# Eight gate tiles of each layer: copied out of PSUM by ScalarE and multiplied with the norm's row on GpSimd, in place of one multiplication on VectorE

## The chip, the cores and the metric

The kernel runs on one core of one Trainium2 chip. The metric is the time of one execution on the device in microseconds (us), given as the median of several runs. The profile speaks of five engines: PE (TensorE's matmuls; PEld is its loading of weights), DVE (VectorE), ACT (ScalarE), POOL (GpSimd) and SP (SyncE, which only issues DMAs here).

## The reference

Two layers, each over 512 tokens of width 1024, all in float32. What matters of one layer:

```
h = rms_norm(x, norm_mix[l])
z = h @ w_in[l]
qa, ka, va, qi, ki, wi, cq, ckv, kr, ga, gb = split_cols(z)
...
y_a = sparse_indexed_attention(qa, ka, va, qi, ki, wi, rel_bias, topk)
...
y_b = latent_attention(qb, kb, vb)
gate_a = jax.nn.sigmoid(ga + b_gate[l, :D_MODEL])
gate_b = jax.nn.sigmoid(gb + b_gate[l, D_MODEL:])
merged = gate_a * (y_a @ w_proj_a[l]) + gate_b * (y_b @ w_proj_b[l])
x = x + merged @ w_out[l]
```

Then comes a convolutional feed-forward block. Mixer a picks 128 keys for each query (top-k over an indexer's scores); mixer b is dense latent attention. Both have eight heads. The second gate, gb, has 1024 channels, that is eight tiles of 128 channels by 512 tokens, and is used only after both mixers.

## The kernel before

Everything is held transposed: channels on the 128 partitions, the 512 tokens along the free dimension. Each float32 factor is split into two float32r parts, high and low, and a product is three matmuls (high by high, high by low, low by high). A `dense` call (L511 to L526) makes one tile of 128 output channels: 24 matmuls into one PSUM bank of tag D, of which there are two, and then a function that empties the bank.

A weight tile arrives raw by SP's DMA (`wr`). ACT casts it to the high part `wh` (L172). The low part `wl` is made in one of two ways: by a subtraction on DVE (L184), or, for gb, ga, kv, uq and some others, by ACT writing the negated copy (L200) and POOL issuing a DMA that adds the raw tile (L201).

The norm is applied late. The matmuls run on x times the gain; the factor of each token, `nrm.row`, the same in all partitions, comes in when a bank is emptied. For both gates that is L686 in `evac_gate`: one DVE multiplication of the bank with the row, written to an SBUF tile. (A branch for gb, switched by `GBL`, is off.) Biases and sigmoid follow at L1254, after mixer a's last head; L906 then multiplies with mixer b's projection.

One generator, `mix_dense`, makes all the projections of a layer in a fixed order: indexer, latents, four gb tiles (`GB_0`), the two groups of mixer b's keys, values and queries (`attn_b`), four more gb tiles, group 0 of mixer a, and so on. The heads of the mixers are woven with it: each step of a head lets this filler advance by a rate. Steps that should come some ticks later are put off by `later(n, f)`; a tick is one step of a generator. Beside that, `top_k` (L991) runs on DVE, alternating MAX8 (L998) and MATCH_REPLACE8 (L1005) over three score tiles, 48 rounds of each a layer. POOL turns the queries of mixer b by their rotary angles (L868 to L874) and adds the bias tiles for mixer a (L1078).

A list scheduler then sets the order in each engine's queue, by a model of when operands are ready and by program order as priority; an instruction marked `keep_in_program_order` is kept in its place in the program. On the chip each queue runs strictly in that order, and an instruction at its head that waits holds what is behind it.

The functions that the change touches are `evac_gate` (L680), the loop over gb at the end of `mix_dense`'s part for mixer b (L893 to L899), and the lines ahead of the sigmoids (L1249 to L1254).

Of the kernel before, what the change touches and what calls it, by code (L numbers as in the profile page):

```python
# [15 lines left out]
OP = mybir.AluOpType  # L16
# [45 lines left out]
PBO = 0  # L62
# [11 lines left out]
SU2 = '12'  # L74
PCH = 2000
GA_0 = 0
GBL = 0
LAG_D = [2, 4, 5, 7, 8, 10, 12]
WPOOL = []
WMOD = 1  # L80
# [153 lines left out]
def trunk(ctx: ExitStack, tc: tile.TileContext, xT, wd, vecs, rel, rot_n, onehot, outT):  # L234
# [12 lines left out]
    def slot(s, dt=F32):  # L247
        return sb.tile([128, 512], dt, name=nm(s), tag="slot", bufs=N_SLOTS)
# [15 lines left out]
    def bank(tag):  # L264
        return ps.tile([128, 512], F32, name=nm(tag), tag=tag, bufs=N_PS[tag])

    mm = nc.tensor.matmul
    V, A, G = nc.vector, nc.scalar, nc.gpsimd
# [5 lines left out]
    def later(n, f):  # L274
        if n == 0:
            f()
        else:
            pending.append((clock[0] + n, f))
# [110 lines left out]
    def vc(l, i, n=1):  # L389
        return vec[:, l * NV + i:l * NV + i + n]  # L390
# [120 lines left out]
    def dense(kt, parts, xh, xl, evac, c0=0, last=True, tag="D", t0=0):  # L511
        h, o = parts
        p = bank(tag)
        c = lambda k: slice(c0 + k * 128, c0 + (k + 1) * 128)
        if "d" in LO:
            seq = [(h[:, c(k)], x[k]) for k in range(kt) for x in (xh, xl)] + [(o[:, c(k)], xh[k]) for k in range(kt)]
        else:
            seq = [q for k in range(kt) for q in ((h[:, c(k)], xh[k]), (h[:, c(k)], xl[k]), (o[:, c(k)], xh[k]))]
        for n, (w, x) in enumerate(seq):
            if n and n % 3 == 0:  # L520
                yield
            mm(p[:, t0:], lhsT=w, rhs=x[:, t0:], start=n == 0, stop=n == len(seq) - 1, skip_group_check=True)  # L522
        if last:
            W.ahead()
        evac(p)
        yield  # L526

    def rows(name, grp, nrm, evac):

        pp = [bank("D").rearrange("p (t c) -> p t c", t=2) for _ in range(2)]  # L530
        for half in range(2):
            h, o = W.get(name, 2 * grp + half)
            for b in range(2):
                for t in range(2):
                    ts = slice((2 * b + t) * 128, (2 * b + t + 1) * 128)
                    c = lambda k: slice(k * 256, (k + 1) * 256)
                    xs = [(nrm.h[4 * half + k][:, ts], nrm.o[4 * half + k][:, ts]) for k in range(4)]
                    if "r" in LO:
                        seq = [(x, h[:, c(k)]) for k in range(4) for x in xs[k]] + [(xs[k][0], o[:, c(k)])
                                                                                for k in range(4)]  # L540
                    else:
                        seq = [q for k in range(4) for q in ((xs[k][0], h[:, c(k)]), (xs[k][1], h[:, c(k)]),
                                                             (xs[k][0], o[:, c(k)]))]
                    for n, (x, w) in enumerate(seq):
                        mm(pp[b][:, t, :], lhsT=x, rhs=w, start=n == 0 and half == 0 and t == 0,  # L545
                           stop=n == 11 and half == 1, skip_group_check=True)
                        if n == 5 or (n == 11 and t == 0):
                            yield
                if b == 1:
                    W.ahead()  # L550
                if half:
                    evac(b, pp[b])
                yield
# [3 lines left out]
    late = []  # L557

    def mix_dense(l, nrm):
# [119 lines left out]

        def evac_gate(name, m, p):  # L680
            g = slot(name)
            if name == "gb" and GBL and not PBO:
                A.copy(g, p)
                late.append((g, nrm.row))
            else:
                tables["v"] = V.tensor_tensor(out=g, in0=p, in1=nrm.row, op=OP.mult)  # L686
            st[name][m] = g
# [89 lines left out]
        def evac_va(grp, b, p):  # L777
            for t in range(2):
                j = 2 * b + t
                d = st["va"][j][grp] = slot("va", F32R)  # L780
                d = d.rearrange("p (h c) -> p h c", c=128)
                split_into(d[:, :, 0:64], d[:, :, 64:128], p[:, t, :].rearrange("p (h c) -> p h c", c=64),
                           nrm.rstd[:, j:j + 1])

        def attn_a(grp):
            yield from heads("qa", grp, None)
            yield from heads("ka", grp, gab[:, 2 * l:2 * l + 1])
            yield from rows("va", grp, nrm, lambda b, p: evac_va(grp, b, p))
            done.add(f"a{grp}")
# [103 lines left out]
        for m in range(8):  # L893
            if m == GB_0:
                yield from attn_b(0)
            if m == GB_1:
                yield from attn_b(1)
            yield from dense(KD, W.get("gb", m), nrm.h, nrm.o, lambda p, m=m: evac_gate("gb", m, p))
        yield from attn_a(0)  # L899
        for m in range(GA_0):  # L900
            yield from dense(KD, W.get("ga", m), nrm.h, nrm.o, lambda p, m=m: evac_gate("ga", m, p))
# [15 lines left out]
        for m in range(GA_0, 8):  # L917
            yield from dense(KD, W.get("ga", m), nrm.h, nrm.o, lambda p, m=m: evac_gate("ga", m, p))
# [241 lines left out]
    nrm = Norm(gain0)  # L1160
# [10 lines left out]
    for l in range(DEPTH):  # L1171
        st.clear()
        done.clear()
        fl = Filler(mix_dense(l, nrm))
        if l:
            for k in range(SQ_DOWN, KD):
# [70 lines left out]
                     lambda h: lambda j: st["va"][j][h // 4][:, (h % 4) * 128:(h % 4 + 1) * 128], each_a, "a")  # L1247
        fl.until("ga")
        gb = st["gb"]  # L1249
        for g, row in late:  # L1250
            V.tensor_tensor(out=g, in0=g, in1=row, op=OP.mult)
        late.clear()
        for m in range(0 if PBO else 8):
            table(AF.Sigmoid, gb[m], gb[m], bias=vc(l, V_GATE + 8 + m))  # L1254

# [28 lines left out]
        nrm = Norm(vc(l, V_FFN, KD))  # L1284
# [203 lines left out]
        nrm = nxt  # L1488
# [103 lines left out]
```

## Time and profile before

| what | value |
|---|---|
| median of 3 runs | 1543.3 us (1542.56 to 1543.44) |
| profiled execution, its own time | 1542.06 us |
| its span, first to last instruction | 1540.3 us |
| around the span | 1.76 us |
| mean granted TensorE clock | 1.000 |
| gb tiles, both layers | 16 |

The profile's page gives for each engine the busy time and its share of the span. A group of instructions is shown by line, engine and operation, what it writes and reads, and the count, then its busy time, the mean of one in nanoseconds, the engine's idle time before it, and what ended that. A row of the timeline has start, length, engine and line; an "x2" at its end means two in a row merged. A row of waits has who waited for whom, the total, the times and the longest. Line numbers of the kernel after are 4 higher than before between L899 and L1249.

### The profile page before, as it was taken

The page shows a single profiled execution, that of the slowest core. Times are in us where ns is not written, and L with a number is a line of the kernel's source. Part 1 is how long each engine was busy: PE and PEld are TensorE (multiplying, and loading weights), DVE is VectorE, ACT ScalarE, POOL GpSimd, SP SyncE. Part 2 cuts the span into 40 slices and gives each one's busy share as a digit, 9 for nine tenths or more (in the row PEclk, how much of TensorE's full clock was granted, in tenths as well). Part 3 has the DMA queues.
Part 4 walks back from the last instruction along what each step waited for, and adds up shares of the span by engine and source line. Part 5 has one row for each costly group of instructions (what it writes and reads, how often), then busy time and mean ns, then how long its engine had stood idle before and what let it go on. Part 6 is the DMA issues. An engine that isn't in the chain of part 4 may idle for free.

```text
span 1540.3 us, 23962 instructions
## 1 busy us (share of the span) xinstructions
PE 1530.1 (99%) x8662; PEld 1336.5 (87%) x8662; DVE 1123.0 (73%) x2301; ACT 947.0 (61%) x1555; POOL 392.7 (25%) x578
## 2 busy tenths in 40 slices
PE   9999999999999999999999999999999999999999
PEld 7887999888888898889998889998888888988899
DVE  7799988666476693447979999886574757835587
ACT  6856677773567545664457577686635765466642
POOL 1243003300011431124602520124001115321255
PEclk9999999999999999999999999999999999999999
DMA  7564134734488438883454641356435883488823
GB/s 277 132 156 123 56 96 97 191 112 134 120 181 200 108 117 213 190 181 93 139 184 110 157 110 56 104 125 168 139 96 142 186 185 95 147 201 193 176 86 109
DMA packets 72983, 219.02 MB, mean 142 GB/s; under 512 B 8528, under 2 KB 10104, under 8 KB 72736
## 3 DMA queue, kind: packets, MB, share of 16 engines
q1 hardware_dynamic: 53824, 149.15, 30.8%
q0 software_dynamic: 18432, 65.28, 23.6%
q10 hardware_dynamic: 608, 3.05, 0.6%
q8 instruction: 68, 1.11, 0.3%
q14 instruction: 51, 0.42, 0.1%
HBM read 143.77 MB, written 6.84 MB: 98 GB/s over the span
## 4 chain that ended last, share of the span: by engine, by line
PE 81%; DVE 9%; ACT 2%; issue 1%; POOL 0%; ACTq 0%
PE D L522 35%; PE T L522 15%; PE D L545 6%; PE L L1385 5%; PE T L1385 4%; PE D L1385 3%; PE Y L1043 2%; PE Y L1385 2%; PE T L1036 2%; PE L L522 2%; DVE sc L1005 1%; DVE m L998 1%; PE L L323 1%; PE L L322 1%; DVE mx L1130 1%
## 5 line engine op out<-in xcount | busy, mean ns | idle before, releaser
L172 ACT CAST wh<-wr 128x1024 fp32r<-128x1024 f32 (+1 forms) x206 | 212.2, 1033 | 161.2 <-PE D L522 67.8
L201 POOL DMA_DIRECT2D wl<-wr x128 | 110.8, 878 | 631.0 <-ACT wl L200 602.3
L522 PE MATMUL D<-hxh,wh 128*128 128x512 f32 (+1 forms) x448 | 176.5, 394 | 0.0
L522 PE MATMUL D<-hxl,wh 128*128 128x512 f32 (+1 forms) x448 | 175.2, 391 | 0.0
L200 ACT ACTIVATE wl<-wr 128x1024 fp32r<-128x1024 f32 (+2 forms) x128 | 132.2, 1035 | 47.2 <-PE D L522 25.0
L190 ACT CAST wh<-wr 128x896 fp32r<-128x896 f32 x88 | 82.8, 942 | 103.7 <-POOL wr L214 62.5
L1078 POOL TENSOR_TENSOR P<-M,sel 128x128 f32<-128x128 f32 (+1 forms) x64 | 54.4, 903 | 272.8 <-DMA M<-skewd 157.6
L522 PE MATMUL D<-hxh,wl 128*128 128x512 f32 (+1 forms) x448 | 119.2, 393 | 0.0
L545 PE MATMUL D<-wh,hxh 128*128 128x256 f32 x384 | 113.9, 297 | 0.0
L214 POOL TENSOR_TENSOR wr<-wr 128x256 f32<-128x256 f32 x88 | 93.9, 1068 | 61.9 <-DVE wr L213 43.3
L545 PE MATMUL D<-wl,hxh 128*128 128x256 f32 x384 | 109.1, 284 | 0.0
L195 DVE TENSOR_TENSOR wl<-wr,wh 128x896 fp32r<-128x896 f32 x88 | 103.4, 1177 | 7.2 <-ACT wh L190 2.9
L545 PE MATMUL D<-wh,hxl 128*128 128x256 f32 x384 | 108.4, 282 | 0.0
L184 DVE TENSOR_TENSOR wl<-wr,wh 128x1024 fp32r<-128x1024 f32 x78 | 97.2, 1251 | 6.7 <-ACT wh L172 6.6
L522 PE MATMUL D<-hrl,wh 128*128 128x512 f32 x256 | 99.6, 389 | 0.0
L522 PE MATMUL D<-hrh,wh 128*128 128x512 f32 x256 | 99.6, 389 | 0.0
L522 PE MATMUL T<-hrl,wh 128*128 128x512 f32 x256 | 99.6, 389 | 0.0
L522 PE MATMUL T<-hrh,wh 128*128 128x512 f32 x256 | 99.6, 389 | 0.0
L522 PEld LDWEIGHTS D<-hxh,wh 128*128 128x128 f32 x448 | 84.4, 188 | 13.6 <-DVE gb L686 0.2
L522 PEld LDWEIGHTS D<-hxl,wh 128*128 128x128 f32 x448 | 84.4, 188 | 12.7
L522 PEld LDWEIGHTS D<-hxh,wl 128*128 128x128 f32 x448 | 81.4, 188 | 13.8
L1329 DVE SCALAR_TENSOR_TENSOR c<-T,vec,c 128x511 f32<-128x511 f32 x32 | 23.9, 748 | 89.1 <-ACT c L1326 89.1
(438 smaller groups left out, 4566.9 us busy)
## 6 DMA issues: line engine op xcount, KB each, us to landing
wr<-in_wd_dram SPq DMA_DIRECT2D x198, 512.0 KB, 3.8
wl<-wr POOLq DMA_DIRECT2D x120, 512.0 KB, 5.4
wr<-in_wd_dram SPq DMA_DIRECT2D x88, 256.0 KB, 2.7
x<-in_xT_dram SPq DMA_DIRECT2D x16, 256.0 KB, 4.5
M<-skewd SPq DMA_DIRECT2D x16, 256.0 KB, 4.0
skewd<-biasd ACTq DMA_DIRECT2D x1, 2560.0 KB, 12.0
kah<-kah SPq DMA_DIRECT2D x16, 128.0 KB, 4.5
kal<-kal SPq DMA_DIRECT2D x16, 128.0 KB, 3.8
```

What stands on the lines that cost most here:

```text
L172: ins = self.nc.scalar.copy(h[:, :n], t[:, :n])
L184: eng.tensor_tensor(out=o[:, c], in0=t[:, c], in1=h[:, c].bitcast(F32), op=OP.subtract)
L190: self.nc.scalar.copy(h[:, :896], t[:, 128:1024])
L195: self.later(lag, lambda: self.nc.vector.tensor_tensor(out=o[:, :896], in0=t[:, 128:1024], in1=h[:, :896].bitcast(F32), op=OP.subtract))
L200: self.nc.scalar.activation(o, t, AF.Copy, scale=-1.0)
L201: self.nc.gpsimd.dma_start(o.bitcast(F32), t, accum_op=OP.add)
L214: g(2)(out=b[:, 6:8], in0=b[:, 0:3:2], in1=b[:, 3:6:2], op=OP.add)
L522: mm(p[:, t0:], lhsT=w, rhs=x[:, t0:], start=n == 0, stop=n == len(seq) - 1, skip_group_check=True)
L545: mm(pp[b][:, t, :], lhsT=x, rhs=w, start=n == 0 and half == 0 and t == 0, stop=n == 11 and half == 1, skip_group_check=True)
L1036: nc.tensor.transpose(p[:, (i - j) * 128:(i - j + 1) * 128], P[:, P0[i] + j * 128:P0[i] + (j + 1) * 128], ident)
L1078: G.tensor_tensor(out=P[:, P0[i]:P0[i] + w], in0=M[:, 512 - w:512], in1=sel[:, SEL0[i]:SEL0[i] + w], op=OP.add)
L1385: mm(p, lhsT=w, rhs=x, start=b0, stop=b1, skip_group_check=True)
```

## The change

`evac_gate` now lets ACT copy a gb bank to its SBUF tile without the row, and notes the tile in `late`. When all eight dense calls of gb have been written, eight multiplications with the row, in place and on POOL, are put in, the first at once and each next one four ticks later (`LAG_B`). They are marked to keep their program order. The multiplications on DVE that stood unused ahead of the sigmoids go. The gate ga is not touched.

```diff
-GBL = 0
+LAG_B = 4
...
         def evac_gate(name, m, p):
             g = slot(name)
-            if name == "gb" and GBL and not PBO:
+            if name == "gb":
                 A.copy(g, p)
-                late.append((g, nrm.row))
+                late.append(g)
             else:
                 tables["v"] = V.tensor_tensor(out=g, in0=p, in1=nrm.row, op=OP.mult)
             st[name][m] = g
...
             yield from dense(KD, W.get("gb", m), nrm.h, nrm.o, lambda p, m=m: evac_gate("gb", m, p))
+        for n, g in enumerate(late):
+            later(LAG_B * n, lambda g=g: tc.keep_in_program_order(
+                G.tensor_tensor(out=g, in0=g, in1=nrm.row, op=OP.mult)))
+        late.clear()
         yield from attn_a(0)
...
         gb = st["gb"]
-        for g, row in late:
-            V.tensor_tensor(out=g, in0=g, in1=row, op=OP.mult)
-        late.clear()
         for m in range(0 if PBO else 8):
```

The scheduler's order follows. First POOL's queue in layer 0, where the second group of mixer b's queries is turned; `wl_1529` and `wl_1534` are the low parts of the weights for the seventh and eighth gb tile, `qn_1265` the last tile of queries. Before:

```order
L874 COPY qn_1265<-lateq 128x4x4
L201 DMA wl_1529<-wr_1242 128x1024
L201 DMA wl_1534<-wr_1244 128x1024
L868 TENSOR_TENSOR rot_1545<-qn_1265,rotn 128x64
L869 TENSOR_TENSOR rot_1545<-qn_1265,rotn 128x64
L870 TENSOR_TENSOR qn_1265<-qn_1265,rotn 128x4x16
L871 TENSOR_TENSOR qn_1265<-qn_1265,rotn 128x4x16
L872 TENSOR_TENSOR qn_1265<-qn_1265,rot_1545 128x4x16
L873 TENSOR_TENSOR qn_1265<-qn_1265,rot_1545 128x4x16
L1078 TENSOR_TENSOR P_2902<-M_2903,sel 128x128
```

And after, the same piece of POOL's queue (the first rows of it, up to the two DMAs and the first turn):

```order
L874 COPY qn_1265<-lateq 128x4x4
L901 TENSOR_TENSOR gb_916<-gb_916,row_444 128x512
L901 TENSOR_TENSOR gb_966<-gb_966,row_444 128x512
L901 TENSOR_TENSOR gb_1008<-gb_1008,row_444 128x512
L901 TENSOR_TENSOR gb_1050<-gb_1050,row_444 128x512
L201 DMA wl_1529<-wr_1242 128x1024
L201 DMA wl_1534<-wr_1244 128x1024
L868 TENSOR_TENSOR rot_1545<-qn_1265,rotn 128x64
```

The first four multiplications stand ahead of the two DMAs and of the last turn; the other four stand behind the last turn and ahead of the first bias tile. In layer 1 two stand ahead of the two DMAs, two inside the last turn, and four behind it.

ACT's queue at the first gb tiles of layer 0 (weight casts, then mixer b's first keys). Before:

```order
L172 CAST wh_959<-wr_778 128x768
L200 ACTIVATE wl_960<-wr_778 128x768
L172 CAST wh_1001<-wr_867 128x384
L200 ACTIVATE wl_1002<-wr_867 128x384
L172 CAST wh_1043<-wr_914 128x1024
L200 ACTIVATE wl_1044<-wr_914 128x1024
L824 COPY kn_1053<-L_1067 128x4x64
```

After:

```order
L683 COPY gb_916<-D_877 128x512
L172 CAST wh_959<-wr_778 128x768
L200 ACTIVATE wl_960<-wr_778 128x768
L683 COPY gb_966<-D_919 128x512
L172 CAST wh_1001<-wr_867 128x384
L200 ACTIVATE wl_1002<-wr_867 128x384
L683 COPY gb_1008<-D_969 128x512
L172 CAST wh_1043<-wr_914 128x1024
L200 ACTIVATE wl_1044<-wr_914 128x1024
L683 COPY gb_1050<-D_1011 128x512
```

One copy stands between each two pairs of weight casts. The four later copies of a layer stand among the exponentials and casts of mixer b's heads. On DVE the sixteen multiplications are gone and the rest moves up, with top-k steps drawn forward by a few places.

## Prediction

> **What bounds the kernel now.** First the page: the span, the engines' busy time and the head of the chain that ended last.
>
> ```profile
> span 1540.3 us, 23962 instructions
> ...
> PE 1530.1 (99%) x8662; PEld 1336.5 (87%) x8662; DVE 1123.0 (73%) x2301; ACT 947.0 (61%) x1555; POOL 392.7 (25%) x578
> ...
> PE 81%; DVE 9%; ACT 2%; issue 1%; POOL 0%; ACTq 0%
> ```
>
> PE is busy for 1530.1 of 1540.3 us. The change takes no matmul away, so it can only win back time in which PE waits, and can only lose by making PE wait. Over the whole span that is 10.2 us of idle time. Next, the stages in which gb is made: one table by window. Its columns are length, then busy time of PE, PEld, DVE, ACT and POOL.
>
> ```profile
> 76.00:97.00 21.00, 21.00 (x98) 17.51 (x97) 21.00 (x64) 7.33 (x11) 3.90 (x8) 1.00 0.60 142
> 97.00:130.00 33.00, 31.84 (x165) 26.63 (x165) 32.73 (x113) 24.44 (x55) 23.86 (x68) 1.00 0.61 146
> 130.00:175.00 45.00, 44.29 (x267) 37.77 (x266) 44.02 (x110) 30.21 (x71) 3.44 (x8) 1.00 0.35 94
> ...
> 860.00:892.00 32.00, 31.47 (x160) 25.89 (x159) 32.00 (x113) 23.68 (x52) 23.08 (x63) 1.00 0.64 152
> 892.00:937.00 45.00, 44.56 (x277) 39.35 (x276) 44.53 (x111) 33.26 (x78) 5.20 (x16) 1.00 0.38 94
> ```
>
> Layer 0's first four gb tiles fall in 76 to 97, mixer b's keys and queries in 97 to 130, the other four gb tiles in 130 to 175; 860 to 937 is the same in layer 1. DVE is full in all of them (32.73 of 33.00 us and so on). Yet PE loses only 1.16 + 0.71 + 0.53 + 0.44 = 2.84 us there: DVE is late, but PE mostly has filler matmuls in between. Where DVE's lateness does reach PE is seen in the waits of PEld, the weight load being the first to stop.
>
> ```profile
> PEld T L1112 <- DVE qn L886: 2.2, 6, 0.6
> PEld L L818 <- DVE vb L302: 2.1, 2, 1.2
> PEld Y L1043 <- DVE ptl L302: 1.8, 6, 0.4
> ...
> PEld T L1036 <- DVE P L1025: 1.0, 2, 0.9
> ```
>
> And for PE itself, once a layer, at mixer b's second keys:
>
> ```profile
> PE L L818 <- DVE vb L302: 1.2, 2, 0.8
> ```
>
> **The change, part by part.** What DVE sheds: the sixteen multiplications, one group, with two neighbours in its timeline.
>
> ```profile
> L686 DVE TENSOR_TENSOR gb<-D,row 128x512 f32<-128x512 f32 x16 | 10.9, 680 | 0.0
> ```
>
> ```profile
> 89.54 0.67 DVE L686 TENSOR_TENSOR gb<-D,row 128x512 f32<-128x512 f32 x1
> 90.13 0.41 DVE L998 MAX8 m<-sc 128x8 f32<-128x256 f32 x1
> ```
>
> Each took 0.68 us, but the next instruction began 0.59 us after it did: 16 x 0.59 = 9.4 us of DVE's queue. Idle time ahead was 0.0, so DVE never waited for these banks; it came late to them. Eight of the sixteen, 4.7 us, go ahead of 97 and 860, before any multiplication runs on POOL. There DVE is 2.4 us earlier in each layer, more than PE's idle time of 1.16 and 0.53 us in the next windows. Not all of that is DVE's doing. I take the two waits for vb, **-1.2 us**; the bounds are -1.7 (both windows' idle time) and 0 (top-k steps fill the gap).
>
> What POOL gains: sixteen multiplications of 128x512. The same shape with two SBUF inputs is the last bias addition of mixer a:
>
> ```profile
> L1078 POOL TENSOR_TENSOR P<-M,sel 128x512 f32<-128x512 f32 x16 | 21.1, 1317 | 0.0
> ```
>
> 1.32 us each, 21.1 us of POOL in all. POOL has the room: in 130 to 175 it is busy for 3.44 of 45.00 us, and it later stands waiting for mixer a's tiles.
>
> ```profile
> POOL P L1078 <- DMA M<-skewd: 157.6, 8, 94.4
> ```
>
> The product is wanted only by the sigmoids, the second row here, from 326.8 us on. The last gb tile of layer 0 leaves its bank at 166, so the later time itself costs nothing.
>
> ```profile
> L686 DVE TENSOR_TENSOR gb<-D,row x16: 669/681/689, 78.1 to 928.9; 128x512 f32<-128x512 f32 x16
> L356 ACT ACTIVATE gb<-gb,vec x16: 707/722/729, 326.8 to 1096.0; 128x512 f32<-128x512 f32 x16
> ```
>
> What POOL's work does to DVE is the real price. Two rows of the timeline, the first with a 128x384 addition and the 128x512 one behind it merged; then the same small DVE step undisturbed:
>
> ```profile
> 240.92 2.04 POOL L1078 TENSOR_TENSOR P<-M,sel 128x384 f32<-128x384 f32 x2
> 241.95 1.04 DVE L333 TENSOR_SCALAR y<-m 128x16 int32<-128x16 int32 x1
> ```
>
> ```profile
> 133.95 0.16 DVE L333 TENSOR_SCALAR y<-mq 128x16 int32<-128x16 int32 x1
> ```
>
> The step that takes 0.16 us took 1.04 beside the second addition, and ended just as that did, at 242.99 against 242.96. That is 0.88 us lost. It isn't so for all of DVE's work. Beside another 128x512 addition on POOL, two MAX8 took no longer than apart from one:
>
> ```profile
> 73.78 1.59 POOL L669 TENSOR_TENSOR sqq<-sqq,sqq 128x512 f32<-128x512 f32 x1
> 73.79 0.88 DVE L998 MAX8 m<-sc 128x8 f32<-128x384 f32 x2
> ...
> 101.12 0.88 DVE L998 MAX8 m<-sc 128x8 f32<-128x384 f32 x2
> ```
>
> So a multiplication costs DVE between 0 and 0.88 us. DVE's queue in 130 to 175 mixes both kinds (top-k, maxima and PSUM reads; rsqrt steps, scalings and weight subtractions), so I take half, 0.44: 16 x 0.44 = 7.0 us, bounds 0 and 14.1. Against that stand 4.7 us shed in the same windows, and 4.7 - 1.2 = 3.5 us of head start that PE had no use for. DVE comes out 1.2 us ahead, and PE notices nothing: **0**. The bounds on the path are -1.15 (the idle time of these windows, 0.71 + 0.44) and 14.1 - 9.4 = +4.7.
>
> What POOL's queue holds back: in layer 0 four multiplications stand ahead of two weight DMAs and the last turn of queries. POOL went straight from the turn to the DMAs; PE's first use of the seventh tile's low part is the third row.
>
> ```profile
> 130.07 1.80 POOL L201 DMA_DIRECT2D wl<-wr  x2 [0.19 <-issue]
> ```
>
> ```profile
> wl<-wr POOLq DMA_DIRECT2D x120, 512.0 KB, 5.4
> ```
>
> ```profile
> 147.91 1.32 PE L522 MATMUL D<-hxh,wl 128*128 128x512 f32 x5
> ```
>
> Four at 1.32 us put the issue at 135.4 and the landing at 140.8, 7.1 us before PE asks. The end of the last turn, and who needs it:
>
> ```profile
> 133.15 0.45 POOL L873 TENSOR_TENSOR qn<-qn,rot 128x64 f32<-128x64 f32 x1
> ...
> 143.87 1.02 DVE L886 TENSOR_TENSOR qn<-qn,y 128x384 f32<-128x384 f32 x2
> ```
>
> The turn, which ended at 133.6, now ends near 138.9; DVE scales the last two query tiles from 143.87, so about 5 us are left. In layer 1 only two multiplications stand ahead of the DMAs. That costs **0**. Without this cover PE would wait for what is missing, microsecond by microsecond.
>
> What ACT gains: sixteen copies out of PSUM. The same copy exists:
>
> ```profile
> L727 ACT COPY raw<-D 128x512 f32<-128x512 f32 x16 | 9.3, 581 | 3.8 <-PE D L545 3.5
> ```
>
> 16 x 0.58 = 9.3 us. The first four of a layer stand between weight casts, where ACT idles for PE anyhow:
>
> ```profile
> 92.76 1.05 ACT L172 CAST wh<-wr 128x1024 fp32r<-128x1024 f32 x1 [3.15 <-PE D L522]
> ```
>
> They are hidden. The other eight stand in front of exponentials and casts that PE's heads await: each holds them for up to 0.58 us, 4.6 in all, bounds 0 and +4.6. A copy also waits for its dense call's last matmul, but it is queued well behind that. As ACT is busy for 30.21 of 45.00 us there and holds 2% of the chain, I take less than a tenth: **+0.4**. The banks come free no later than from the late DVE.
>
> Sum: -1.2 + 0 + 0 + 0.4 = -0.8 us. The span goes to 1539.5, the profiled execution from 1542.06 to 1541.3, and the median from 1543.3 to **1542.5 us**, 0.05%. About 0.2%, 3.1 us, is what a measurement here can tell from no change, so I call this the same.
>
> **The rivals.** *DVE is held up by POOL.* If a DVE step of the exposed kind comes up during every multiplication, DVE loses 14.1 us and wins 9.4. It is full in these windows, so nothing absorbs the 4.7 us, and the four back to back in layer 0 fall in front of the maxima that the heads start from. That gives 1548.0. It turns to slower beyond (9.4 + 3.1) / 16 = 0.78 us a multiplication. For it: the full DVE. Against: the filler in PE's order, and the MAX8 rows. Chance 0.14. [...]
>
> *DVE's relief reaches PE in full.* The four DVE rows of PEld's waits add up to 7.1 us; PE's idle time in the windows is 2.8. Between them lies -5.0, so 1538.3. For it: chains through DVE at 9%. Against: relief is spent on top-k steps moved forward. Chance 0.19.
>
> *The multiplication isn't late enough.* The scheduler put four of them into the busiest part of POOL's queue, not between the heads. If the four took 12.4 us rather than 5.3 (3.1 each), the seventh tile's weights would miss PE and both layers would lose about 2 us: 1547. The longest row of that shape quoted is 1.59. Chance 0.04.
>
> **How the numbers follow.** The forecast has 0.63, the rivals 0.19, 0.14 and 0.04. Faster by over 0.2% is the second rival, 0.19; slower is the first and third, 0.18; the same is 0.63. The range takes in all that counts as the same (1540.2 to 1546.4) and reaches most of the way to the two large rivals, 1538.3 and 1548.0: 1539.0 to 1547.0, with about one in ten outside at each end.
>
> **What would show it.** Right: no L686 row with gb; sixteen POOL rows near 1.2 to 1.6 us; DVE rows of about 1 us beside them at L333, L342, L344 or L1025; PE's idle time in 97 to 130 below 1.16 and the wait of L818 for vb shorter; POOL's DMAs near 135. Wrong: PE's idle time in 130 to 175 or 892 to 937 above 2 us with DVE as releaser (first rival), PE idle near 0 in all four windows with DVE below full (second), or PE waiting for a wl DMA (third). A wait of PE for ACT's pth or P behind a gb copy would mean that ACT's term was too small.

## The result, and the profile after

The change made the kernel slower: 1561.1 us (median of four, 1559.86 to 1562.15) against 1543.0 for the kernel before in the same comparison, a ratio of 1.0117 (95% interval 1.010 to 1.0135). That is 18.1 us more; the prediction had 0.8 less, and its range ended at 1547.0. The profiled execution took 1562.15 us for a span of 1560.4.

The page of the profile after, the lines that answer to those of before:

```profile
span 1560.4 us, 23983 instructions
...
PE 1537.3 (99%) x8662; PEld 1340.7 (86%) x8662; DVE 1131.4 (73%) x2285; ACT 954.5 (61%) x1571; POOL 419.8 (27%) x594
...
PE 74%; DVE 12%; ACT 3%; issue 1%; DMA 1%; POOL 0%; DVEq 0%; ACTq 0%; SPq 0%
```

DVE has 16 instructions fewer and is busy for longer, 1131.4 instead of 1123.0 us. PE's idle time went from 10.2 to 23.1 us, and PE itself is busy for 7.2 us more with the same 8662 matmuls. The table by window says where (length, then PE, PEld, DVE, ACT, POOL, the granted clock):

```profile
97.00:130.00 33.00, 31.96 (x160) 26.27 (x159) 33.00 (x113) 24.19 (x57) 22.52 (x63) 1.00 0.62 153
130.00:175.00 45.00, 39.85 (x212) 32.80 (x209) 42.49 (x95) 28.85 (x66) 17.07 (x24) 0.92 0.31 82
...
860.00:892.00 32.00, 30.29 (x144) 25.83 (x143) 32.00 (x108) 21.32 (x48) 15.76 (x47) 1.00 0.69 162
892.00:937.00 45.00, 40.02 (x214) 32.79 (x213) 44.35 (x111) 29.22 (x65) 22.98 (x41) 0.96 0.42 106
```

In the two windows with the multiplications PE now idles for 5.15 and 4.98 us (0.71 and 0.44 before). The granted clock, 1.00 in every window before, is 0.92 and 0.96 there. PE's waits, the four longest:

```profile
PE L L1131 <- ACT P L356: 6.7, 2, 4.3
PE Y L1047 <- DVE ptl L302: 3.1, 6, 1.1
PE L L818 <- DVE vb L302: 2.3, 2, 1.7
PE T L1040 <- DVE y L344: 2.2, 1, 2.2
```

The first names ACT, but ACT waits for DVE. Here is layer 0 on POOL, then on DVE: the four multiplications as one merged row, and the small step of mixer b's query norm (`mq`, L880) that comes up in the middle of them.

```profile
131.82 5.05 POOL L901 TENSOR_TENSOR gb<-gb,row 128x512 f32<-128x512 f32 x4
136.79 1.67 POOL L201 DMA_DIRECT2D wl<-wr  x2
```

```profile
133.85 3.05 DVE L880 SCALAR_TENSOR_TENSOR mq<-ssq,ms 128x16 f32<-128x16 f32 x1
...
138.20 0.17 DVE L1022 RECIPROCAL rs<-sm 128x4 f32<-128x4 f32 x1
```

The step begins at 133.85, during the second multiplication, and ends at 136.90, when the fourth does (136.87). It was let in neither after the second nor after the third. Behind it in DVE's queue stands the reciprocal that ACT needs, and behind ACT stands PE:

```profile
138.40 0.72 ACT L1027 ACTIVATE P<-P,rs 128x512 f32<-128x512 f32 x1 [2.75 <-DVE rs L1022]
139.03 0.35 ACT L356 ACTIVATE P<-L,mx 128x128 f32<-128x128 f32 x1
```

```profile
136.77 0.39 PE L522 MATMUL D<-hxl,wh 128*128 128x512 f32 x1
139.52 0.50 PE L1131 MATMUL L<-tbh,tbh 100*128 100x512 f32 x1 [2.36 <-ACT P L356]
...
142.78 1.09 PE L1040 MATMUL T<-ident,P 128*128 128x128 f32 x4 [2.24 <-DVE y L344]
```

PE's queue has no filler left at this place. The second wait, for `y`, comes from two more DVE steps: L344 was held until the end of the turn (140.16), L343 until that of the fifth multiplication (142.00).

```profile
138.82 1.38 DVE L344 SCALAR_TENSOR_TENSOR y<-t,y 128x16 f32<-128x16 f32 x1
...
140.80 1.23 DVE L343 SCALAR_TENSOR_TENSOR t<-t,mq 128x16 f32<-128x16 f32 x1
```

In layer 1 the step L880 took 4.77 us; there two of the multiplications stand among the last turn's short instructions. DVE, then two rows of POOL:

```profile
907.59 4.77 DVE L880 SCALAR_TENSOR_TENSOR mq<-ssq,ms 128x16 f32<-128x16 f32 x1
```

```profile
910.51 1.77 POOL L901 TENSOR_TENSOR gb<-gb,row 128x512 f32<-128x512 f32 x1
911.74 0.83 POOL L872 TENSOR_TENSOR qn<-qn,rot 128x64 f32<-128x64 f32 x1
```

The step ends at 912.36, when that multiplication does (912.28), though the turn's last two instructions still follow at once. So a step isn't always held to the very end of an unbroken piece of POOL's queue. Its wait begins beside two DMA issues (907.00 to 908.68); what held it there isn't shown.

The other price is the clock; a table by window around the two stalls:

```profile
136.90:140.30 3.40, 1.04 (x5) 0.49 (x3) 3.40 (x13) 1.90 (x5) 3.25 (x8) 1.00 0.72 135
140.30:147.10 6.80, 4.56 (x15) 3.67 (x15) 6.46 (x15) 1.94 (x6) 1.40 (x1) 0.50 0.96 248
...
911.70:915.10 3.40, 0.15 (x1) 0.15 (x2) 3.40 (x17) 1.27 (x4) 1.13 (x3) 1.00 1.04 241
915.10:918.50 3.40, 3.40 (x11) 2.72 (x12) 3.40 (x9) 3.39 (x8) 1.07 (x1) 0.50 0.56 180
```

After 3.4 us in which PE worked for 1.04 or 0.15, the granted clock was half (0.50) for 6.8 and 3.4 us. From 144.09 one matmul of L522 began 0.42 us after the other, at full clock from 135.61 it was 0.23. By an estimate from these rows, PE's work in the two stretches, 4.56 and 3.40 us, would have taken half as long at full clock: about 4.0 us lost. That the stalls brought the fall about is my reading; it wasn't tried by itself. A third stretch at half clock, of 3.4 us, begins at 31 us in this execution, ahead of all that the change touches, and before that one PE had worked for 3.0 of 3.4 us; what set it off is open. Why the four times fall into two pairs (1559.9 and 1560.3, 1561.9 and 1562.2) isn't shown either: the mean granted clock is 0.996 in all four.

### The profile page after: what moved, and what is told of

Read it like the earlier page. It is cut to its first block, busy times and chain, and to the rows that moved or that the text cites. A ratio compares the mean times of both kernels' runs of the same rounds, so it can differ in the third digit from the quotient of the medians.

```text
span 1560.4 us, 23983 instructions
## 1 busy us (share of the span) xinstructions
PE 1537.3 (99%) x8662; PEld 1340.7 (86%) x8662; DVE 1131.4 (73%) x2285; ACT 954.5 (61%) x1571; POOL 419.8 (27%) x594
## 3 DMA queue, kind: packets, MB, share of 16 engines
q10 hardware_dynamic: 608, 3.05, 0.6%
## 4 chain that ended last, share of the span: by engine, by line
PE 74%; DVE 12%; ACT 3%; issue 1%; DMA 1%; POOL 0%; DVEq 0%; ACTq 0%; SPq 0%
PE D L522 33%; PE T L522 15%; PE D L545 6%; PE L L1386 4%; PE T L1386 3%; PE D L1386 2%; PE Y L1047 2%; PE L L522 2%; PE Y L1386 2%; PE T L1040 2%; DVE sc L1009 2%; DVE m L1002 1%; DMA wr<-in_wd_dram 1%; DVE wl L195 1%; DVE mx L1134 1%
## 5 line engine op out<-in xcount | busy, mean ns | idle before, releaser
L522 PE MATMUL D<-hxh,wh 128*128 128x512 f32 (+1 forms) x448 | 177.5, 396 | 0.0
L522 PE MATMUL D<-hxl,wh 128*128 128x512 f32 (+1 forms) x448 | 175.9, 393 | 0.0
L522 PE MATMUL D<-hxh,wl 128*128 128x512 f32 (+1 forms) x448 | 121.5, 396 | 0.0
L214 POOL TENSOR_TENSOR wr<-wr 128x256 f32<-128x256 f32 x88 | 98.8, 1124 | 56.8 <-DVE wr L213 38.3
L184 DVE TENSOR_TENSOR wl<-wr,wh 128x1024 fp32r<-128x1024 f32 x78 | 100.1, 1288 | 9.3 <-ACT wh L172 8.2
L522 PE MATMUL D<-hrl,wh 128*128 128x512 f32 x256 | 99.6, 389 | 0.0
L522 PE MATMUL D<-hrh,wh 128*128 128x512 f32 x256 | 99.6, 389 | 0.0
L522 PE MATMUL T<-hrh,wh 128*128 128x512 f32 x256 | 99.6, 389 | 0.0
L522 PE MATMUL T<-hrl,wh 128*128 128x512 f32 x256 | 99.6, 389 | 0.0
L522 PEld LDWEIGHTS D<-hxh,wh 128*128 128x128 f32 x448 | 84.8, 189 | 13.4
L522 PEld LDWEIGHTS D<-hxl,wh 128*128 128x128 f32 x448 | 84.8, 189 | 13.0
L522 PEld LDWEIGHTS D<-hxh,wl 128*128 128x128 f32 x448 | 81.6, 190 | 13.5
```

The costliest lines, as they stand in the source:

```text
L184: eng.tensor_tensor(out=o[:, c], in0=t[:, c], in1=h[:, c].bitcast(F32), op=OP.subtract)
L214: g(2)(out=b[:, 6:8], in0=b[:, 0:3:2], in1=b[:, 3:6:2], op=OP.add)
```

## The experiments

Theory A: the multiplications on GpSimd hold VectorE, one waiting step through a whole train of them, and PE waits behind that. (A train is a row of POOL's instructions that follow one another at once.) Rival B: it is ScalarE's copies. Rival C: each multiplication costs VectorE about its length wherever it stands. All times are medians; each difference is to the kernel before in the same comparison (1542.7, 1543.2, 1543.4 and 1542.7 us for the runs e1 to e4, e5 to e8, e9 to e12, e13 and e14). In e1, e3 to e6, e8 and e12 to e14 PE, ACT and DVE run the change's own order row for row, and only POOL's differs; e2 has the order of before on all of them but POOL. Where a run puts the product elsewhere or leaves its place empty (e1, e3, e4, e9 to e11), the change's loop over `late` goes; the excerpts of e3, e4 and e9 show only the rest.

**e1, the copies alone.**

```diff
-        for n, g in enumerate(late):
-            later(LAG_B * n, lambda g=g: tc.keep_in_program_order(
-                G.tensor_tensor(out=g, in0=g, in1=nrm.row, op=OP.mult)))
         late.clear()
```

> This kernel has ScalarE's sixteen copies, but leaves the multiplication with the norm's row out altogether (gb goes into the sigmoid without it). Theory A, the multiplications on GpSimd hold VectorE: without them nothing is lost, VectorE keeps its relief of 9.4 us, and the time is 1538 to 1543, at full clock, with PE idle below 1.2 us in 130 to 175. Rival B, ScalarE's copies stand in front of the heads' exponentials: the loss stays, 1555 or more. Between 1546 and 1552 both would have a part.

1546.9 us, 4.2 more (ratio 1.0023, 1.0013 to 1.0032), clock 1.00. That is at the lower end of the range in which both would have a part: most of the loss goes with the multiplications, but what is left is a loss, not a gain (e7 says whether it is the copies'). PE's waits in e1:

```profile
PE L L818 <- DVE vb L302: 2.3, 2, 1.7
PE Y L1044 <- DVE ptl L302: 2.2, 3, 1.5
```

The wait for vb, which DVE's relief was to end, has grown from 1.2 to 2.3.

**e2, the multiplications alone.**

```diff
-                A.copy(g, p)
+                tables["v"] = V.tensor_tensor(out=g, in0=p, in1=nrm.row, op=OP.mult)
                 late.append(g)
```

> VectorE empties gb's banks with the row as before, no copies on ScalarE; GpSimd's sixteen multiplications are added all the same (so gb carries the row twice). Theory A: the loss is there without any copy, 18 us or more, as VectorE hasn't its relief either: 1558 to 1572, with a VectorE step of 3 us or more beside the train. Rival B: 1543 to 1546, since only the copies cost.

1551.6 us, 8.9 more (1.0058, 1.0043 to 1.0073). A loss without any copy, so B falls as the main cause; but half of what A had said. The train and the step held, from e2's timeline of POOL and of DVE:

```profile
130.37 5.04 POOL L901 TENSOR_TENSOR gb<-gb,row 128x512 f32<-128x512 f32 x4
```

```profile
133.30 2.15 DVE L880 SCALAR_TENSOR_TENSOR mq<-ssq,ms 128x16 f32<-128x16 f32 x1
```

The step comes up later in the train and is held until its end again (135.45 against 135.41). In the profiled execution, 1550.55 us, the stalls brought no fall of the clock (1.00); two of the four executions have a mean clock of 0.996 and took 1552.6 and 1553.4 us.

As the change and e1 differ in POOL's order alone, the multiplications cost 18.1 - 4.2 = 13.9 us in the change's order; in that of before they cost 8.9. With PE's order the same, the traces also say where. From matmul to matmul the change falls 6.7 us behind e1 at layer 0's train and 4.8 at layer 1's; e2 falls 2.8 and 2.1 behind before. So the difference arises at the two trains. The rows above put about 4.0 us down to the clock; the longest waits themselves are longer too (6.7 + 2.2 us, against 2.6 + 1.9 + 1.2 in e2). The exact shares weren't tried by themselves.

**e3, each multiplication right behind its copy**, so that they don't follow one another.

```diff
                 A.copy(g, p)
-                late.append(g)
+                later(1, lambda g=g: tc.keep_in_program_order(
+                    G.tensor_tensor(out=g, in0=g, in1=nrm.row, op=OP.mult)))
```

> Copies and the same sixteen multiplications, each put one tick behind its own copy, so that no four stand back to back. Theory A (what costs is the train: one waiting VectorE step is held until the whole train is over): each hits VectorE for at most 1.3 us, the longest small step on VectorE is about 1.3 instead of 3.05 and 4.77, PE's filler takes it in, 1541 to 1547. Rival C (every multiplication costs VectorE about its whole length wherever it stands): no better than the change, 1555 to 1561.

1549.7 us, 7.0 more (1.0047, 1.0032 to 1.0062): above the figures of A, but 2.9 more than the copies alone where the change has 13.9. The same sixteen multiplications cost a fifth when spread out: C falls. (Their neighbours differ as well as their spacing; e5, e8 and e12 look at the train itself.)

**e4, one multiplication with each head of mixer a.**

```diff
                     P, ahead = (ahead if h else first_a), (bias_a(h + 1) if h < 7 else None)
+                    tc.keep_in_program_order(G.tensor_tensor(out=late[h], in0=late[h], in1=nrm.row, op=OP.mult))
```

> Copies as in the change; the multiplications are moved to mixer a, one with each head, behind that head's predecessor's bias additions on GpSimd, 175 us and later. Theory A: outside the stage in which VectorE is full the blocks have a cover; the relief of 9.4 us stays: 1538 to 1544. Rival C: sixteen blocks of 1.3 us are 21 us of VectorE in a stage with room, of which a part reaches PE: 1545 to 1552. Rival B: 1555 or more, the copies being the same.

1566.7 us, 24.0 more (1.0157, 1.0142 to 1.0172), worse than the change: my forecast for A was wrong by over 20 us. Its timeline at 315 us, POOL and DVE, says why:

```profile
314.69 1.29 POOL L1221 TENSOR_TENSOR gb<-gb,row 128x512 f32<-128x512 f32 x1
315.93 0.84 POOL L201 DMA_DIRECT2D wl<-wr  x1
316.53 3.29 POOL L1078 TENSOR_TENSOR P<-M,sel 128x128 f32<-128x128 f32 x4
319.55 2.70 POOL L1221 TENSOR_TENSOR gb<-gb,row 128x512 f32<-128x512 f32 x2
```

```profile
317.23 6.11 DVE L184 TENSOR_TENSOR wl<-wr,wh 128x1024 fp32r<-128x1024 f32 x1
323.27 0.54 DVE L302 TENSOR_TENSOR ptl<-T,pth 128x384 fp32r<-128x384 f32 x1
```

A weight subtraction (1.21 us elsewhere) stood from 317.23 until 1.1 us after the train of six had ended, and mixer a's `ptl` behind it; PE waited for that for 4.4 us. The four bias additions were a train already, and the multiplications made it longer. "A stage with room" was the wrong way to look: what counts is who shares a train.

**e5, quarters.** Each multiplication as four of 128x128, in the same places.

```diff
+            for c in range(0, 512, 128):
+                later(LAG_B * n, lambda g=g[:, c:c + 128], r=nrm.row[:, c:c + 128]: tc.keep_in_program_order(
+                    G.tensor_tensor(out=g, in0=g, in1=r, op=OP.mult)))
```

> The change with every multiplication cut into four of 128x128, in the same places of GpSimd's queue, so that a train is sixteen short instructions instead of four long ones. Theory A (VectorE isn't let in between GpSimd instructions that follow at once): the small VectorE step is again held for 3 us or more, and the time stays near the change's, 1555 to 1565. Rival D (the block lasts one GpSimd instruction): no step is held for more than about 0.5 us, and the time falls to 1547 to 1552, near that of the products spread out.

1561.1 us, 17.9 more (1.0117, 1.0104 to 1.0131), as the change. POOL and DVE:

```profile
130.87 6.29 POOL L902 TENSOR_TENSOR gb<-gb,row 128x128 f32<-128x128 f32 x15
```

```profile
132.89 4.30 DVE L880 SCALAR_TENSOR_TENSOR mq<-ssq,ms 128x16 f32<-128x16 f32 x1
```

The step comes up in the fifth of the fifteen instructions of 0.42 us and is held for 4.30 us, through ten more, to 137.19, the end of the train (137.16). The block wasn't one of a single instruction here: rival D falls.

**e6, filling instead of multiplying** (the product is left out).

```diff
-                G.tensor_tensor(out=g, in0=g, in1=nrm.row, op=OP.mult)))
+                G.memset(g, 0.0)))
```

> The multiplication is left out and GpSimd instead fills gb's tile with zeros (a 128x512 MEMSET, which reads nothing) in the same places of its queue. Theory A, in the form that the block is one of reading from SBUF: no VectorE step is held, time as with the copies alone, 1545 to 1549. Rival E (any GpSimd instruction that touches SBUF holds VectorE): steps are held beside the MEMSETs and the time stays above 1551, less than the change only as far as MEMSETs are shorter.

1546.3 us, 3.1 more (1.0018, 1.0009 to 1.0027): as the copies alone. But a MEMSET took 0.56 us, and layer 0's four were over before L880 came up, so this didn't tell reading from length; e13 does.

**e7, sixteen copies too many.**

```diff
                 tables["v"] = V.tensor_tensor(out=g, in0=p, in1=nrm.row, op=OP.mult)
+            if name == "gb":
+                A.copy(g, g)
```

> The kernel before, with the row multiplied by VectorE out of PSUM as ever and VectorE's order as it was, but with sixteen more copies on ScalarE (gb's tile onto itself). It parts the 4 us that the copies alone cost: if it was ScalarE's time, 1545.5 to 1548; if it was VectorE's order, in which top-k steps moved ahead of mixer b's values, 1542 to 1543.5.

1543.7 us, ratio 1.0004 (0.9994 to 1.0013), 0.2 above the range given for the order. ScalarE's time cost nothing that could be measured here, with DVE's order as before but for two rows. So e1's 4 us belong most likely to the order that the scheduler makes once DVE's sixteen instructions are gone. (These copies read SBUF, the change's read PSUM.)

**e8 and e12, gaps in the train.** A small MEMSET after each multiplication; in e8 onto a new tile, in e12 onto one that existed.

```diff
+            later(LAG_B * n, lambda: tc.keep_in_program_order(G.memset(gain0, 0.0)))
```

> The change with one 128x16 MEMSET on GpSimd between every two multiplications: an instruction that reads nothing from SBUF. [...] If the train counts as one as long as GpSimd's queue runs on, it stays at 1557 to 1564.

> The train with a small MEMSET between the multiplications once more, now onto a tile that exists already (gain0, not read any more), so that no tile lies elsewhere than in the change. [...] If the MEMSETs themselves had made the earlier run with gaps slower than the change: 1566 to 1571, with the feed-forward stage slower again. Theory A in its plain form (no letting in at all): 1559 to 1564.

e8 took 1570.5 us (1.0172, 1.0159 to 1.0186), e12 1557.2 (1.0089, 1.0075 to 1.0103). e8 lies above the 1557 to 1564 of a train that counts as one, e12 below the 1559 to 1564 of no letting in at all. e8 is no clean test, as its feed-forward stages were slower too (last section). In e12 the step L880 of layer 0 was let in where POOL writes, at the MEMSET of 133.11 (POOL, then DVE):

```profile
131.89 1.28 POOL L901 TENSOR_TENSOR gb<-gb,row 128x512 f32<-128x512 f32 x1
133.11 0.10 POOL L902 MEMSET gain<- 128x8 f32 x1
133.17 1.30 POOL L901 TENSOR_TENSOR gb<-gb,row 128x512 f32<-128x512 f32 x1
```

```profile
132.62 0.58 DVE L880 SCALAR_TENSOR_TENSOR mq<-ssq,ms 128x16 f32<-128x16 f32 x1
...
904.01 4.02 DVE L333 TENSOR_SCALAR y<-mq 128x16 int32<-128x16 int32 x1
```

0.58 us instead of 3.05. In layer 1 the MEMSETs did not help: the last row was held for 4.02 us through two MEMSETs, two multiplications and most of the turn. It is another kind of step, a TENSOR_SCALAR, and in e13 L333 was held beside MEMSETs too (0.82 us instead of 0.16), which speaks for the kind; but in layer 0 of e12 one was let in at the end of a MEMSET, after 0.75 us, so kind and place aren't fully parted.

**e9 to e11, is the relief worth something if the order is held?** In the change's order 58 top-k steps stand ahead of the first vb of layer 0, 52 before. e9 is e1 with each round's first MAX8 kept in its place; e10 has e3's multiplications besides; e11 has them on VectorE before the sigmoids.

```diff
                     ins = V.max(out=m8[i], in_=st["sc"][i][:, :128 * (i + 1)])
+                    if i == 3:
+                        tc.keep_in_program_order(ins)
```

> The copies alone again (the row's multiplication left out), but the first MAX8 of every top-k round is held at its place in the program, so that VectorE's order has as many top-k steps ahead of mixer b's values as before (53 instead of 58 in layer 0, 149 instead of 156 in layer 1; before: 52 and 150). If the 4 us that the copies alone cost come from those steps, the wait for vb falls to 0.8 us or less a layer and the time to 1540 to 1544. If they come from something else in the copies, it stays at 1545 to 1548.

> Complete again: the copies, each multiplication on GpSimd behind its copy, and the top-k held as in the run without the products. Both parts of the theory together (spread products cost about 3 us, the drawn-forward top-k about 4): 1543 to 1547, against 1549.7 without the hold. If the hold does nothing: 1548 to 1551.

> Complete: the copies on ScalarE, no product on GpSimd; VectorE multiplies with the row after mixer b, before the sigmoids; top-k held. If VectorE's relief in the full stage is worth something, this is where it shows: 1539 to 1543. If PE has no use for it, 1543 to 1546, and no kernel of this kind beats the one before.

e9 took 1550.0 us (1.0045, 1.0033 to 1.0058), e10 1552.6 (1.0061, 1.0047 to 1.0075) and e11 1553.6 (1.0067, 1.0054 to 1.0081). All three missed. In e9 no single wait for vb is above 0.5 us any more, yet the kernel is slower than e1:

```profile
PE Y L1046 <- DVE ptl L302: 1.3, 1, 1.3
...
PE T L1115 <- DVE qao L316: 1.0, 3, 0.5
PE L L818 <- DVE vb L302: 0.9, 3, 0.3
```

The hold did bring the top-k steps ahead of the first vb down to 53, and the waits only moved. But e9 is no clean test of those steps: with the hold the scheduler planned anew, and DVE's order in e9 lies farther from that of before than e1's does (about 610 rows stand elsewhere, against about 240). Which rows of the new order cost the 4 us stays open, and I found no version that beats the kernel before. e10 less e9 gives 2.6 us for spread multiplications, as e3 less e1 did.

**e13 and e14, reading or length?** Three MEMSETs for each multiplication; and one copy of the tile onto itself (the product is left out of both).

```diff
+            for _ in range(3):
+                later(0 if n < 4 else LAG_B * n, lambda g=g: tc.keep_in_program_order(G.memset(g, 0.0)))
```

```diff
+                G.tensor_copy(out=g, in_=g)))
```

> The multiplication left out; three 128x512 MEMSETs in a row on each gb tile, so that GpSimd writes for as long as it multiplied (3 x 0.48 us where a multiplication took 1.3), with nothing read. If reading is what holds VectorE (theory A): no VectorE step of 128x16 is held for more than about 1 us, 1545 to 1550. If what counts is how long GpSimd keeps its queue full, whatever it does: steps held for 2 us and more, 1553 to 1562.

> The row left out; GpSimd copies each gb tile onto itself (one SBUF input, 128x512) in the very places of the multiplications. Theory A with 'any read holds': steps of 128x16 held for as long as the train of copies lasts; if a copy takes as long as a multiplication 1557 to 1562, if it is shorter, less in proportion (at half the length about 1551 to 1555). If only two inputs on GpSimd collide with two on VectorE: as with the copies alone, 1545 to 1549.

e13: 1548.5 us (1.0037, 1.0023 to 1.0050), with 27.8 us of MEMSETs, more than the change's 25.1 of multiplications. In layer 1 eleven stand in a row, and DVE goes through its steps beside them; the first row of DVE is the step L880 a little earlier, where MEMSETs stand among the turn's instructions (POOL, then DVE):

```profile
903.77 6.59 POOL L901 MEMSET gb<- 128x512 f32 x11
```

```profile
901.92 0.33 DVE L880 SCALAR_TENSOR_TENSOR mq<-ssq,ms 128x16 f32<-128x16 f32 x1
...
904.40 0.16 DVE L343 SCALAR_TENSOR_TENSOR t<-t,mq 128x16 f32<-128x16 f32 x1
...
904.76 0.60 DVE L1029 TENSOR_SCALAR P<-P,rs 128x256 f32<-128x256 f32 x1
...
908.44 1.21 DVE L184 TENSOR_TENSOR wl<-wr,wh 128x1024 fp32r<-128x1024 f32 x1
```

Beside the eleven, steps with two SBUF inputs took 0.16 and 1.21 us, as in the change's trace where POOL stands still (0.16 at 143.71, 1.21 at 144.34). Only the TENSOR_SCALAR was slower (0.60 against 0.34); another, L333, took 0.82 instead of 0.16 us, until the end of a MEMSET. In layer 0 the four were again over when L880 came up, but layer 1 is enough. e14: 1550.3 us (1.0048, 1.0030 to 1.0066), 0.7 below the range for copies of half the length; a copy was 0.57 us long in the train, under half a multiplication, and in layer 1, where copies stand among the turn's instructions, L880 was held for 2.28 us:

```profile
901.06 2.28 DVE L880 SCALAR_TENSOR_TENSOR mq<-ssq,ms 128x16 f32<-128x16 f32 x1
```

At the same place it took 0.33 us with MEMSETs in e13, and 0.61 in the kernel before, where the turn stands alone. It wasn't let in during either of two copies, so here GpSimd instructions with one input read from SBUF were enough to hold it; this rests on one step.

## Why the prediction was wrong, step by step

- **DVE's relief, -1.2.** Wrong in sign. The wait for vb grew from 1.2 to 2.3, and the copies without the product cost 4.2 us (e1). I treated the rest of the order as fixed and wrote that it "moves up"; the scheduler planned PE, ACT and DVE anew, and that order is worse by itself. With e7 that is the likeliest reading; which of its rows cost the time is open.
- **The collision term, taken at 0.** This is the step that failed. "A multiplication costs DVE between 0 and 0.88 us" took its bound from one row in which a step met the last addition of a train. The step that came up inside a train waited for several instructions: 3.05 and 4.77 us. The trace of before had this already, with L880 itself, which was held through the turn until its end at 133.60:

```profile
132.74 0.90 DVE L880 SCALAR_TENSOR_TENSOR mq<-ssq,ms 128x16 f32<-128x16 f32 x1
```

  And "PE notices nothing" offset sums over a window, relief against loss; but the loss came in two places, all at once, in front of the steps that the heads wait for, where no filler stood in PE's queue. Measured: 13.9 us in the change's order, of which about 4.0 by the clock; 8.9 in the order of before (e2).
- **The clock.** Missing altogether: it was 1.00 in all windows of before, whose longest wait quoted is 0.8 us, and I did not ask what a longer one would do. About 4.0 us by the rows.
- **POOL's queue, 0.** Right: the DMAs were issued at 136.79 (I had 135.4), and PE never waits for a `wl` in the list of its waits above.
- **ACT, +0.4.** Right as far as e7 goes: +0.6, interval about -0.9 to +2.0.
- **The rivals.** "DVE is held up by POOL" named the mechanism, the place and the sign, at a chance of 0.14, and its 4.7 us were the same undersized bound. The evidence quoted against this rival, two MAX8 undisturbed beside an addition, was true and beside the point: one exposed step was enough, since DVE's queue stood still behind it, for 3.05 us in layer 0 and 4.77 in layer 1. That PE has filler was true on average and false at L1131; the same matmul waited for ACT in the kernel before too, for 0.4 us.

## What to carry to other kernels

Before moving work to GpSimd, look for VectorE steps of the kinds held here (L880 for 3.05 and 4.77 us, L184 for 6.11 instead of 1.21) that come up beside it, and price them by the whole unbroken piece of GpSimd's queue, neighbours included, not by one instruction. Try such instructions spread out (here 2.9 us instead of 13.9 for the same sixteen), and beware of appending them to a train that exists (e4: 24.0 us). An engine's sum over a window says little about the end time: ask which single instruction is late, who waits for it, and whether anything stands between.

## What the runs showed of the hardware that I had not expected

In these runs a VectorE step with two SBUF inputs was mostly not let in between GpSimd instructions that read SBUF and followed at once: L880 was held for 4.30 us through the last eleven of fifteen of 0.42 (e5), and L184, a step of 1.21 us, took 6.11 (e4). In the change's profiled execution 3.4 us in which PE worked for 1.04 were followed by 6.8 us at half clock; by the estimate above, the clock cost about 4.0 us beside PE's waits for P and for y, 6.7 and 2.2 us. The length of a wait alone doesn't seem to tell: in the profiled executions e2, with a longest wait of 2.6 us, kept a clock of 1.00, while e14, with a longest of 1.8, has a mean of 0.997 (in which stretches it fell isn't shown here). And e8's new tile of 64 bytes a partition went with slower matmuls far from the change. From 350 to 700 us, in e8 and then in e12:

```profile
L522 PE MATMUL D<-hrl,wh 128*128 128x512 f32 x112 | 44.4, 397 | 0.0
```

```profile
L522 PE MATMUL D<-hrl,wh 128*128 128x512 f32 x119 | 46.3, 389 | 0.0
```

Matmul for matmul, e8 fell another 5.9 us behind e12 from 350 to 708 us and 5.5 from 1127 to 1475: most of the 13 us between the two kernels. The tiles' places in SBUF differ, and little else does; that they do it wasn't tried by itself.
